# State-space work in short steps between projection blocks, half the output map on GpSimd, and low-part DMAs queued with the low phase

## The chip, the cores and the metric

The kernel runs on one core of one Trainium2 chip. The metric is the device time of one execution in microseconds (us). A core has five engines that each work through a queue of their own in order: TensorE (PE in the profile, its weight loads PEld), VectorE (DVE), ScalarE (ACT), GpSimd (POOL) and SyncE (SP), which here only issues DMAs. An instruction that waits holds up everything behind it on its engine.

## The reference, cut to what matters

One batch of 512 time steps by 1024 channels goes through two layers. Each layer is `x + rms_norm(mixer(rms_norm(x)))`. The change lies in the first layer, whose mixer is:

```python
p = u @ ev_w_in                       # 1024 -> 5120
a_in, a_z, b_val, b_gate, b_z = split(p)          # 1024 columns each
ya = s5_layer(a_in, ...)              # 64 groups of 16 channels, 64 complex states each
ya = gelu(ya); ya = ya * sigmoid(ya @ s5_w_glu + s5_b_glu); ya = ya * silu(a_z)
yb = conformer_conv(b_val, b_gate, ...)           # val*sigmoid(gate), causal conv of 31 taps,
yb = yb * silu(b_z)                               # LayerNorm, swish, pointwise 1024 x 1024
y = concatenate([ya, yb]) @ ev_w_out
```

The state-space part is, per group, `s_t = Lbar * s_(t-1) + Bbar u_t`, `y_t = Re(C s_t) + D u_t`. The second layer is a chunked gated linear attention, which the change leaves alone. Everything is float32.

## The kernel before

**Blocks.** A projection block makes 128 output channels for all 512 steps: 24 matmuls of 128x512 (`mm_st`). Float32 accuracy comes from splitting weights and activations into a high and a low part. A block has a high phase (`wh` times high and low activation, 16 matmuls, L186 and L187) and then a low phase (`wl` times the high activation, 8 matmuls, L189). The first layer's input map has 40 such blocks: 8 for the state-space input (called a here), 8 values (v), 8 gates (g), and 8 each of the two branch gates (zb, za).

**Weights.** For each block SP loads the raw weight (`wraw`, L118, three buffers). ACT writes its negative into `wl` (L130, three buffers), a DMA issued by POOL adds `wraw` to the rounded high part that is still to be taken off (L131, an accumulating DMA, called the low-part DMA here), and ACT makes `wh` (L143, two buffers). ACT also empties the blocks' PSUM banks (three) and issues nothing; a block can start when its `wh` is there and its low phase when the low-part DMA has landed.

**State-space chunks.** The 64 groups go in 8 chunks of 8. `s5_prep(c)` makes a chunk's matrices: the input map `bmt` and `bm` (three two-input operations by `outer`, L528, L530, L532, for each of two halves, on DVE for chunks 0 and 1 and on POOL for the others; then transposes, L544), the response `kt` (L551, L554, L555, L557), the output map `cme` (`outer` again, on DVE, both halves), and for each second chunk the phases (`phases`, six operations on POOL, L507 to L509). It loads `cb` (L519), and ACT makes `csp` and `ci` of it (L522, L523; one `ci` buffer). `s5_in(c)` loads the chunk's input `u` and runs the scan on DVE (L588 to L615), `s5_out(c)` multiplies out `ya` (L628 to L643). The parameters behind all chunks (`s5_params`, powers in `pr`, `prb`, `wb`) are worked out at the start, the last of them on POOL (L398 to L401).

**Order.** A scheduler lays out every engine's queue from priorities and from times that it simulates; `feed()` raises a priority, `background()` lowers it (for the convolution, 31 operations of DVE per chunk, L655 and L656). The program's order sets the rest: 8 a blocks, then `s5_prep` of chunks 0 and 1 and `s5_in(0)`, and then eight rounds. Round c runs `s5_in(c+1)`, `s5_prep(c+2)` and `s5_out(c)` in turn and then four blocks: v, g, zb, za of channel block c. After the rounds come the half-GLU map, the convolution's LayerNorm (it ends in `xbh`), the pointwise map and the output map, and the second layer.

Of the kernel before, what the change touches and what calls it, by code (L numbers as in the profile page):

```python
# [51 lines left out]
def trunk(ctx: ExitStack, tc: tile.TileContext, A: dict, out: bass.AP, dbg: dict | None = None):  # L52
# [58 lines left out]
    wst = {"next_raw": 0, "next_split": 0, "raw": {}, "hl": {}, "low": {}}  # L111
# [10 lines left out]
    def w_low(i, dst=None):  # L122


        while wst["next_raw"] <= i:
            w_raw()
        l = wpool.tile([P, 1024], F32R, tag="wl", bufs=3, name=f"wl{i}") if dst is None else dst
        raw = wst["raw"][i]
        with feed():
            SC.activation(l, raw, AF.Copy, scale=-1.0)  # L130
            G.dma_start(l.bitcast(F32), raw, accum_op=ALU.add)  # L131
        wst["low"][i] = l

    def w_split(dst=None):
        i = wst["next_split"]
        while wst["next_raw"] <= i:
            w_raw()
        if i in dma_low and i not in wst["low"]:
            w_low(i, dst and dst[1])
        raw = wst["raw"].pop(i)  # L140
        h = wpool.tile([P, 1024], F32R, tag="wh", bufs=2, name=f"wh{i}") if dst is None else dst[0]
        with feed():
            SC.copy(h, raw)  # L143
# [23 lines left out]
    def w_get():  # L167
        i = wcur[0]
# [12 lines left out]
    def mm_st(acc, w, xh, xl):  # L181
        wh, wl = w
        whv = wh.rearrange("p (k c) -> p k c", c=P)
        wlv = wl.rearrange("p (k c) -> p k c", c=P)
        for k in range(KT):
            PE.matmul(acc, whv[:, k, :], xh[:, k, :], start=(k == 0), stop=False)  # L186
            PE.matmul(acc, whv[:, k, :], xl[:, k, :], start=False, stop=False)  # L187
        for k in range(KT):
            PE.matmul(acc, wlv[:, k, :], xh[:, k, :], start=False, stop=(k == KT - 1))  # L189
# [96 lines left out]
    SY.dma_start(par, A["s5p"])  # L286
# [205 lines left out]
    def phases(c):  # L492

        sh = [P, GC, 8, 8]
        ws = slice(c // 2 * GC, c // 2 * GC + GC)
# [8 lines left out]
        for o, (a, b, op) in enumerate(((0, 1, ALU.subtract), (1, 0, ALU.add))):
            r_ = h5.tile(sh, F32, tag=f"ph{o}", bufs=1, name=f"ph{o}_{c}")
            wt = h5.tile(sh, F32, tag="wt", bufs=1, name=f"wt{o}_{c}")
            G.tensor_tensor(out=r_, in0=w1(0), in1=w0(a), op=ALU.mult)  # L507
            G.tensor_tensor(out=wt, in0=w1(1), in1=w0(b), op=ALU.mult)
            G.tensor_tensor(out=r_, in0=r_, in1=wt, op=op)  # L509
            out_.append(r_.rearrange("p g a b -> p (g a b)"))  # L510
        pair[c // 2] = out_

    def s5_prep(c):
# [3 lines left out]
        gs = slice(g0_, g0_ + GC)  # L517
        cb = h5.tile([P, 4, GC, GP], F32, tag="cb", bufs=2, name=f"cb{c}")
        SY.dma_start(cb, A["s5cb"][c])  # L519
# [3 lines left out]
        SC.mul(ci_, cb[:, 1], -1.0)  # L523
# [10 lines left out]
        bm = q5.tile([P, GC, P], F32, tag="bm", bufs=2, name=f"bm{c}")  # L534
        cme = q5.tile([P, GC, TB, GP], F32, tag="cme", bufs=3, name=f"cme{c}")
        kt = q5.tile([P, GC, GP], F32, tag="kt", bufs=2, name=f"kt{c}")
        for h in range(2):
            hs = slice(h * 4, h * 4 + 4)
            bmt = q5.tile([P, 4, GP, TB], F32, tag="bmt", bufs=2, name=f"bmt{c}")
            pt1 = h5.tile([P, 4, GP, TB], F32, tag="wt", bufs=1, name=f"pt1_{c}")  # L540
            outer(pe_, bmt, pt1, h, prb, cb[:, 2, hs], cb[:, 3, hs], 2)
            tp = ps("aux")
            for j in range(4):
                PE.transpose(tp[:, j * P:(j + 1) * P], bmt[:, j].rearrange("p q s -> p (q s)"), ident)  # L544
            with feed():
                SC.copy(bm[:, hs, :], tp.rearrange("p (g n) -> p g n", n=P))
            yield

            kp = ps("aux")
            for j in range(4):  # L550
                PE.matmul(kp[32 * j:32 * j + 32, 0:P], cr_[:, h * 4 + j, :], bmt[:, j].rearrange("p q s -> p (q s)"), start=True, stop=True)  # L551
            ks = q5.tile([P, P], F32, tag="ks", bufs=2, name=f"ks{c}")
            with feed():
                SC.copy(ks, kp[:, 0:P])  # L554
            PE.transpose(kp[:, P:2 * P], ks, ident)  # L555
            with feed():
                V.tensor_tensor(out=kt[:, hs, :], in0=kp[:, P:2 * P].rearrange("p (g q) -> p g q", q=32)[:, :, 0:GP],  # L557
                                in1=dg[:, g0_ + h * 4:g0_ + h * 4 + 4, :], op=ALU.add)
# [7 lines left out]

        if c % 2 == 0:
            phases(c)
        half = slice(c % 2 * NS, c % 2 * NS + NS)
        ct_, st_ = (h5.tile([P, S], F32, tag=n, bufs=2, name=f"{n}{c}") for n in ("ct", "st"))  # L570
        for dst, src in zip((ct_, st_), pair[c // 2]):
            for r_ in range(2):
                SY.dma_start(dst[r_ * NS:r_ * NS + NS], src[half])
        prep[c] = (bm, cme, tm, ct_, st_)
# [84 lines left out]
    for c in range(KT):  # L659
# [3 lines left out]
        with feed():  # L663
            ai = tmp((P, TB, NB))
            SC.copy(ai, acc.rearrange("p (b s) -> p s b", s=TB))
            SY.dma_start(u_d[c], ai)

    def value_gate(c):
        w = w_get()
        av = ps()  # L670
        mm_st(av, w, uh, ul)
        w = w_get()
        ag = ps()
        mm_st(ag, w, uh, ul)
        h = hpool.tile([P, 30 + S], F32, tag="h", name=f"h{c}")
        G.memset(h[:, 0:30], 0.0)
        with feed():
            sg = tmp()
            SC.activation(sg, ag, AF.Sigmoid)  # L679
            V.tensor_mul(h[:, 30:30 + S], av, sg)  # L680
        htile[c] = h
        with background():
            conv(c)
# [3 lines left out]
    def gate_z(dst):  # L687
        w = w_get()
        acc = ps()
        mm_st(acc, w, uh, ul)  # L690
        with feed():
            sg = tmp()
            SC.activation(sg, acc, AF.Silu)
            SY.dma_start(dst, sg)

    def run(g, n=1):
        for _ in range(n):
            next(g)

    for c in range(2):  # L700
        run(s5_prep(c), 5)
    run(s5_in(0), 2)
    for c in range(KT):
        nx = s5_in(c + 1) if c + 1 < KT else iter([None] * 2)
        pre = s5_prep(c + 2) if c + 2 < KT else iter([None] * 5)
        cur = s5_out(c)
        run(nx)
        run(pre, 2)
        run(nx)
        run(cur)  # L710
        run(pre, 2)
        run(cur)
        run(pre)
        value_gate(c)
        gate_z(zb_d[c])
        gate_z(za_d[c])
# [500 lines left out]
```

## Time and profile before

| | us |
|---|---|
| median of 3 executions | 945.14 (944.32 to 946.32) |
| the profiled execution, its own time | 946.38 |
| span of its profile | 944.7 |
| PE busy | 897.7 (95%) |
| DVE busy | 641.9 (68%) |
| ACT busy | 485.1 (51%) |
| POOL busy | 245.4 (26%) |

A row of the timeline is the start, the duration, the engine, the line, and the tiles, with the idle time of the engine just before and what ended it in brackets. A row of a table by windows is the stretch of time, its length, the busy time of the engines named, the TensorE clock granted (1.00 is full speed), the mean share of the 16 DMA engines, and the bytes they moved. A row of a table of waits names who waited for what: the total, how often, and the longest. Stages of PE's work, by its own rows: the first 8 blocks run from 17 to 64.24 us, the blocks and chunks of the rounds from there to 320.10, the half-GLU map and the beginning of the output map up to 413.00, then the pointwise map, the rest of the output map, and the second layer.

### The profile page before, as it was taken

The page shows a single profiled execution, that of the slowest core. Times are in us where ns is not written, and L with a number is a line of the kernel's source. Part 1 is how long each engine was busy: PE and PEld are TensorE (multiplying, and loading weights), DVE is VectorE, ACT ScalarE, POOL GpSimd, SP SyncE. Part 2 cuts the span into 40 slices and gives each one's busy share as a digit, 9 for nine tenths or more (in the row PEclk, how much of TensorE's full clock was granted, in tenths as well). Part 3 has the DMA queues.
Part 4 walks back from the last instruction along what each step waited for, and adds up shares of the span by engine and source line. Part 5 has one row for each costly group of instructions (what it writes and reads, how often), then busy time and mean ns, then how long its engine had stood idle before and what let it go on. Part 6 is the DMA issues. An engine that isn't in the chain of part 4 may idle for free. (4 is left out here: it accounts for less than half of the span.)

```text
span 944.7 us, 12134 instructions
## 1 busy us (share of the span) xinstructions
PE 897.7 (95%) x4396; PEld 718.9 (76%) x4396; DVE 641.9 (68%) x1206; ACT 485.1 (51%) x693; POOL 245.4 (26%) x258
## 2 busy tenths in 40 slices
PE   5995998999999999999999979999999999999996
PEld 4873776777778877778887758888888888888875
DVE  7953999999989989832579477584483232744546
ACT  6542786786678855564444566343543242523430
POOL 2693657463123422011054002000200020000222
PEclk8998999999999999999999979999999999999998
DMA  9877987787988885288463112212212223324412
GB/s 278 228 198 194 229 199 184 178 205 204 215 220 228 210 231 179 92 224 201 153 215 124 45 63 93 84 37 82 90 67 90 73 83 135 134 89 164 193 45 89
DMA packets 54955, 142.74 MB, mean 151 GB/s; under 512 B 14256, under 2 KB 15792, under 8 KB 54896
## 3 DMA queue, kind: packets, MB, share of 16 engines
q1 hardware_dynamic: 46832, 112.62, 35.9%
q0 software_dynamic: 8064, 29.36, 17.3%
q8 instruction: 34, 0.56, 0.2%
q14 instruction: 25, 0.20, 0.1%
HBM read 95.18 MB, written 13.22 MB: 115 GB/s over the span
## 5 line engine op out<-in xcount | busy, mean ns | idle before, releaser
L143 ACT CAST wh<-wraw 128x1024 fp32r<-128x1024 f32 x126 | 132.1, 1048 | 161.4 <-PE ps_mm L801 92.5
L149 DVE TENSOR_TENSOR wl<-wraw,wh 128x1024 fp32r<-128x1024 f32 x70 | 87.0, 1243 | 115.2 <-ACT wh L143 114.8
L655 DVE SCALAR_TENSOR_TENSOR ps_cv<-h,cw,ps_cv 128x512 f32<-128x512 f32 x232 | 161.7, 745 | 2.7 <-ACT ps_cv L652 1.8
L186 PE MATMUL ps_mm<-u0h,wh 128*128 128x512 f32 x320 | 129.9, 407 | 1.0 <-ACT tmp L679 0.7
L187 PE MATMUL ps_mm<-u0l,wh 128*128 128x512 f32 x320 | 129.4, 405 | 0.0
L800 PE MATMUL ps_mm<-wh,u1h 128*128 128x512 f32 x240 | 96.2, 402 | 3.5 <-ACT wh L143 3.4
L801 PE MATMUL ps_mm<-wh,u1l 128*128 128x512 f32 x240 | 96.3, 401 | 0.8 <-DVE u1l L194 0.8
L131 POOL DMA_DIRECT2D wl<-wraw x56 | 48.9, 884 | 182.4 <-ACT wl L130 178.2
L802 PE MATMUL ps_mm<-wl,u1h 128*128 128x512 f32 x240 | 91.6, 401 | 1.6 <-DVE wl L149 1.6
L189 PE MATMUL ps_mm<-u0h,wl 128*128 128x512 f32 x320 | 82.5, 395 | 1.1 <-DMA wl<-wraw 1.1
L186 PEld LDWEIGHTS ps_mm<-u0h,wh 128*128 128x128 f32 x320 | 61.8, 193 | 16.4 <-issue 1.6
L130 ACT ACTIVATE wl<-wraw 128x1024 fp32r<-128x1024 f32 x56 | 59.2, 1057 | 25.8 <-DMA wraw<-in_w_in_dram 14.0
L187 PEld LDWEIGHTS ps_mm<-u0l,wh 128*128 128x128 f32 x320 | 61.7, 193 | 13.9 <-issue 1.1
L189 PEld LDWEIGHTS ps_mm<-u0h,wl 128*128 128x128 f32 x320 | 59.4, 188 | 14.9 <-DMA wl<-wraw 1.5
L800 PEld LDWEIGHTS ps_mm<-wh,u1h 128*128 128x128 f32 x240 | 45.9, 191 | 14.9 <-ACT wh L143 3.8
L971 POOL TENSOR_TENSOR rg<-rg,ng 128x512 f32<-128x512 f32 x16 | 24.2, 1544 | 124.6 <-ACT rg L970 124.6
L802 PEld LDWEIGHTS ps_mm<-wl,u1h 128*128 128x128 f32 x240 | 45.6, 191 | 13.1 <-DVE wl L149 2.3
L801 PEld LDWEIGHTS ps_mm<-wh,u1l 128*128 128x128 f32 x240 | 45.9, 191 | 11.7 <-DVE u1l L194 1.2
L186 PE MATMUL ps_mm<-u1h,wh 128*128 128x512 f32 x128 | 50.7, 396 | 0.0
L187 PE MATMUL ps_mm<-u1l,wh 128*128 128x512 f32 x128 | 50.5, 394 | 0.0
L1062 POOL TENSOR_TENSOR kr<-kr,fac 128x384 f32<-128x384 f32 x8 | 6.7, 837 | 124.2 <-DVE rr L205 65.1
L800 PE MATMUL ps_mm<-wh,oth 128*128 128x512 f32 x96 | 37.8, 396 | 0.5 <-ACT wh L143 0.5
(341 smaller groups left out, 1993.6 us busy)
## 6 DMA issues: line engine op xcount, KB each, us to landing
wl<-wraw POOLq DMA_DIRECT2D x56, 512.0 KB, 6.1
wraw<-in_w_in_dram SPq DMA_DIRECT2D x40, 512.0 KB, 5.2
wraw<-in_w_out_dram SPq DMA_DIRECT2D x32, 512.0 KB, 3.3
wraw<-in_w_vr_dram SPq DMA_DIRECT2D x32, 512.0 KB, 3.2
wraw<-in_w_qk_dram SPq DMA_DIRECT2D x16, 512.0 KB, 3.3
tm<-kt_d SPq DMA_DIRECT2D x8, 512.0 KB, 6.3
wraw<-in_w_glu_dram SPq DMA_DIRECT2D x8, 512.0 KB, 5.8
wraw<-in_w_pw_dram SPq DMA_DIRECT2D x8, 512.0 KB, 5.1
```

The costliest lines, as they stand in the source:

```text
L130: SC.activation(l, raw, AF.Copy, scale=-1.0)
L131: G.dma_start(l.bitcast(F32), raw, accum_op=ALU.add)
L143: SC.copy(h, raw)
L149: V.tensor_tensor(out=l, in0=raw, in1=h.bitcast(F32), op=ALU.subtract)
L186: PE.matmul(acc, whv[:, k, :], xh[:, k, :], start=(k == 0), stop=False)
L187: PE.matmul(acc, whv[:, k, :], xl[:, k, :], start=False, stop=False)
L189: PE.matmul(acc, wlv[:, k, :], xh[:, k, :], start=False, stop=(k == KT - 1))
L655: V.scalar_tensor_tensor(out=acc, in0=h[:, k:k + S], scalar=cw[:, c, k:k + 1], in1=acc, op0=ALU.mult, op1=ALU.add)
L800: PE.matmul(accs[tt], xh[:, kt, ts_], whj, start=(first and j == 0), stop=False)
L801: PE.matmul(accs[tt], xl[:, kt, ts_], whj, start=False, stop=False)
L802: PE.matmul(accs[tt], xh[:, kt, ts_], wlj, start=False, stop=(last and j == 1))
L971: G.tensor_tensor(out=r_, in0=r_, in1=ng, op=ALU.mult)
```

## The change

1. The blocks' order. It was a0 to a7 and then v, g, zb, za per round. It is now a0, a1, v0, g0, a2 to a7, zb0, za0, and then v, g, zb, za for the channel blocks 1 to 7.
2. `s5_prep` is cut into six steps (first input map; its transposes and the `ci` and `csp` of ACT; the response, second input map, first output map; turned response, second transposes, phases; second response, second output map, loading the phases; second turned response and `tm`), and `s5_in` gets a step of its own for its load. After six blocks these steps run one block apart; then come rounds with 2, 2, 2, 3, 3, 4, 4, 4 blocks.
3. The second half of the output map is made by GpSimd for chunks 2 to 7 (three operations a chunk).
4. The low-part DMA is ordered behind the last matmul of a block's high phase. The dependency is one of order for the scheduler; it adds no semaphore.
5. Cosine and sine of the phases share a tile, so two DMAs of 64x1024 load them for a chunk where four of 64x512 did.
6. The state-space parameters are loaded between the second and the third tile of x, not behind the vectors.
7. `ci` has two buffers, the response and the turned response a PSUM bank each.

```diff
+    order0 = [("a", 0), ("a", 1), ("v", 0), ("g", 0)] + [("a", j) for j in range(2, 8)] + [("zb", 0), ("za", 0)]
+    for j in range(1, 8):
+        order0 += [("v", j), ("g", j), ("zb", j), ("za", j)]
...
         with feed():
-            SC.activation(l, raw, AF.Copy, scale=-1.0)
-            G.dma_start(l.bitcast(F32), raw, accum_op=ALU.add)
+            SC.activation(l, wst["raw"][i], AF.Copy, scale=-1.0)
         wst["low"][i] = l
+        wst["add"].append((i, l, wst["raw"][i]))
+
+    def w_add(after=None):
+
+        for i, l, raw in wst["add"]:
+            with feed():
+                d = G.dma_start(l.bitcast(F32), raw, accum_op=ALU.add)
+            if after is not None:
+                tc.add_manual_dep(d.ins, after.ins.name, mybir.DependencyInfo(mybir.DependencyClass.NoSync, mybir.DependencyReason.DATA), reason="w_add")
+        wst["add"] = []
...
-            PE.matmul(acc, whv[:, k, :], xl[:, k, :], start=False, stop=False)
+            last = PE.matmul(acc, whv[:, k, :], xl[:, k, :], start=False, stop=False)
+        w_add(last)
...
         SY.dma_start(x_t[tt], A["x"][tt * P:(tt + 1) * P, :])
+        if tt == 1:
+            SY.dma_start(par, A["s5p"])
...
-        ci_ = h5.tile([P, GC, GP], F32, tag="ci", bufs=1, name=f"ci{c}")
...
+        def output_map(h):
+            eng = G if h and c >= DVE_PREP else V
+            pt2 = h5.tile([P, 4, TB, GP], F32, tag="wt", bufs=1, name=f"pt2_{c}") if eng is G else q5.tile([P, 4, TB, GP], F32, tag="pt", bufs=1, name=f"pt2_{c}")
+            outer(eng, cme[:, hs[h]], pt2, h, pr, cr_[:, hs[h], 0:GP], ci_[:, hs[h]], 3)
+
+        input_map(0)
+        yield
...
+        ci_ = h5.tile([P, GC, GP], F32, tag="ci", bufs=2, name=f"ci{c}")
+        turn(0)
+        SC.activation(cr_[:, :, 0:GP], cb[:, 0], AF.Copy, scale=sgn)
+        SC.mul(ci_, cb[:, 1], -1.0)
+        yield
...
+        ks = response(0)
+        input_map(1)
+        output_map(0)
+        yield
+        turn_response(0, ks)
+        turn(1)
+        if c % 2 == 0:
+            phases(c)
+        yield
+        ks = response(1)
+        output_map(1)
...
+    blocks(6)
+    run(P_[0])
+    blocks()
+    run(P_[0])
+    blocks()
+    run(P_[0])
+    blocks()
+    run(P_[0], P_[1], I_[0])
+    blocks()
+    run(P_[0], P_[1])
+    blocks()
+    run(P_[0], I_[0], P_[1])
+    blocks()
+    run(I_[0], P_[1])
+    blocks(2)
+    run(P_[1], P_[2], I_[1])
+    blocks(2)
     for c in range(KT):
...
+        n = (2, 2, 2, 3, 3, 4, 4, 4)[c]
+        run(O_[c], nx, p1, p2)
+        blocks(n - n // 2 - n // 3)
+        run(nx, p2, O_[c])
+        blocks(n // 3)
+        run(p2)
+        blocks(n // 2)
+        run(p2, p3)
+        if c + 2 < KT:
+            run(I_[c + 2])
```

Three places show what this does to the queues. The first is POOL's queue at the start, where the low-part DMAs (wl3 belongs to the fourth block) stand among the parameter work (`ya`, `s5ph` and `wb` are its tiles). Before:

```order
L131 DMA wl2_478<-wraw2_469 128x1024
L131 DMA wl3_513<-wraw3_476 128x1024
L398 TENSOR_TENSOR ya_87<-s5ph1_350 128x64
L399 TENSOR_TENSOR ya_87<-s5ph1_350 128x64
L131 DMA wl4_548<-wraw4_511 128x1024
L400 TENSOR_TENSOR s5ph2_351<-ya_87 128x32
L401 TENSOR_TENSOR s5ph2_351<-ya_87 128x32
```

Of the change, from eight operations further on in the same parameter work:

```order
L410 TENSOR_TENSOR ya_87<-s5ph4_352 128x64
L411 TENSOR_TENSOR ya_87<-s5ph4_352 128x64
L412 TENSOR_TENSOR wb_96<-ya_87 128x32
L136 DMA wl3_529<-wraw3_492 128x1024
L413 TENSOR_TENSOR wb_96<-ya_87 128x32
L410 TENSOR_TENSOR ya_87<-wb_96 128x64
L411 TENSOR_TENSOR ya_87<-wb_96 128x64
L136 DMA wl4_564<-wraw4_527 128x1024
L412 TENSOR_TENSOR wb_96<-ya_87 128x32
```

The DMA of wl3 was ahead of the parameter work and stands 11 operations into it. The same holds a block later for wl5 (before behind the second L398 and L399 on `wb`, now ten operations later) and for wl6 and wl7.

The second place is POOL's queue in the middle of the rounds, where it makes phases (`ph`, `wt`) and the input maps (`bmt3`). Before:

```order
L509 TENSOR_TENSOR ph0_2_1065<-ph0_2_1065,wt0_2_1066 128x512
L508 TENSOR_TENSOR wt1_2_1071<-wb_96 128x512
L131 DMA wl13_1221<-wraw13_1184 128x1024
L509 TENSOR_TENSOR ph1_2_1070<-ph1_2_1070,wt1_2_1071 128x512
L530 TENSOR_TENSOR pt1_3_1274<-prb_95,cb3_1265 128x512
L131 DMA wl14_1384<-wraw14_1219 128x1024
L528 TENSOR_TENSOR bmt3_1273<-prb_95,cb3_1265 128x512
```

Of the change:

```order
L520 TENSOR_TENSOR ph2_1421<-ph2_1421,wt0_2_1422 128x512
L519 TENSOR_TENSOR wt1_2_1426<-wb_96 128x512
L136 DMA wl17_1254<-wraw17_1217 128x1024
L520 TENSOR_TENSOR ph2_1421<-ph2_1421,wt1_2_1426 128x512
L535 TENSOR_TENSOR pt2_2_1506<-pr_94,ci2_1323 128x512
L537 TENSOR_TENSOR cme2_1384<-cme2_1384,pt2_2_1506 128x512
L535 TENSOR_TENSOR pt1_3_1516<-prb_95,cb3_1513 128x512
L533 TENSOR_TENSOR cme3_1624<-pr_94,csp1_455 128x512
```

The operations on `cme` are the half of the output map that DVE had. They stand between the phases and the input map of the next chunk, and chunk 2 gets there four blocks later than before (wl17 for wl13).

The third place is ACT's queue around the `ci` of chunk 3, which needs the load of `cb3`. Before:

```order
L554 COPY ks0_818<-ps_aux_813 128x128
L522 ACTIVATE csp0_454<-cb2_956,sgn_74 128x8x16
L546 COPY bm1_850<-ps_aux_858 128x512
L130 ACTIVATE wl11_1117<-wraw11_1083 128x1024
L523 ACTIVATE ci3_1267<-cb3_1265 128x128
L143 CAST wh11_1182<-wraw11_1083 128x1024
L554 COPY ks1_869<-ps_aux_864 128x128
```

Of the change:

```order
L128 ACTIVATE wl12_961<-wraw12_900 128x1024
L562 COPY ks0_938<-ps_aux_933 128x128
L583 ACTIVATE csp0_454<-cb2_1206,sgn_74 128x8x16
L553 COPY bm1_947<-ps_aux_949 128x512
L584 ACTIVATE ci3_1560<-cb3_1513 128x128
L152 CAST wh12_1027<-wraw12_900 128x1024
L723 ACT_TABLE_LOAD
L723 ACTIVATE tmp_989<-ps_mm_963 128x512
```

Both queues have `ci3` directly ahead of a weight's high part, wh11 before and wh12 in the change (blocks are counted from 0). The response copy `ks1` stood right behind them; in the change it comes after another emptied block.

More of the change, by code (lines that the diff above doesn't have):

```diff
@@ L110, in trunk @@
                     wlist.append(A["w_out1"][n, (h - 2) * 4 + j])
-    wst = {"next_raw": 0, "next_split": 0, "raw": {}, "hl": {}, "low": {}}
+    wst = {"next_raw": 0, "next_split": 0, "raw": {}, "hl": {}, "low": {}, "add": []}
     def w_raw():
@@ L139, in w_split @@
             w_low(i, dst and dst[1])
+        if any(a[0] == i for a in wst["add"]):
+            w_add()
         raw = wst["raw"].pop(i)
@@ L167, in w_get @@
     def w_get():
+        w_add()
         i = wcur[0]
@@ L532, in outer, with input_map, turn, response @@
             eng.tensor_tensor(out=o, in0=o, in1=pt, op=ALU.add)
[L534 to L538, printed above, removed]
+        hs = [slice(0, 4), slice(4, 8)]
+        bmts = []
+        def input_map(h):
             bmt = q5.tile([P, 4, GP, TB], F32, tag="bmt", bufs=2, name=f"bmt{c}")
             pt1 = h5.tile([P, 4, GP, TB], F32, tag="wt", bufs=1, name=f"pt1_{c}")
-            outer(pe_, bmt, pt1, h, prb, cb[:, 2, hs], cb[:, 3, hs], 2)
+            outer(pe_, bmt, pt1, h, prb, cb[:, 2, hs[h]], cb[:, 3, hs[h]], 2)
+            bmts.append(bmt)
+        def turn(h):
             tp = ps("aux")
             for j in range(4):
-                PE.transpose(tp[:, j * P:(j + 1) * P], bmt[:, j].rearrange("p q s -> p (q s)"), ident)
+                PE.transpose(tp[:, j * P:(j + 1) * P], bmts[h][:, j].rearrange("p q s -> p (q s)"), ident)
             with feed():
-                SC.copy(bm[:, hs, :], tp.rearrange("p (g n) -> p g n", n=P))
-            yield
+                SC.copy(bm[:, hs[h], :], tp.rearrange("p (g n) -> p g n", n=P))
+        def response(h):
             kp = ps("aux")
             for j in range(4):
-                PE.matmul(kp[32 * j:32 * j + 32, 0:P], cr_[:, h * 4 + j, :], bmt[:, j].rearrange("p q s -> p (q s)"), start=True, stop=True)
+                PE.matmul(kp[32 * j:32 * j + 32, 0:P], cr_[:, h * 4 + j, :], bmts[h][:, j].rearrange("p q s -> p (q s)"), start=True, stop=True)
             ks = q5.tile([P, P], F32, tag="ks", bufs=2, name=f"ks{c}")
@@ L565, in s5_prep @@
         SY.dma_start(tm, bass.AP(tensor=kd.tensor, offset=kd.offset, ap=[[(2 * TB - 1) * P, GP], [P, TB], [1, TB * P]]))
[L567 to L574, printed above, removed]
+        tms[c] = tm
         yield
+    tms = {}
     state = {}
@@ L615, in s5_in @@
         V.tensor_tensor(out=sv[:, :, 1:NB], in0=zv[:, :, 0:NB - 1], in1=zsv[:, :, 0:NB - 1], op=ALU.subtract)
-        state[c] = (u, sv, tm, cme)
+        state[c] = (u, sv, cme)
         yield
     def s5_out(c):
-        u, sv, tm, cme = state.pop(c)
+        (u, sv, cme), tm = state.pop(c), tms.pop(c)
         yp_ = ps("aux")
@@ L656, in conv, with block @@
         V.scalar_tensor_tensor(out=h[:, 30:30 + S], in0=h[:, 30:30 + S], scalar=cw[:, c, 30:31], in1=acc, op0=ALU.mult, op1=ALU.add)
-    for c in range(KT):
+    half_glu = {}
+    def block(n, c):
         w = w_get()
@@ L662, in trunk @@
         mm_st(acc, w, uh, ul)
[L663 to L683, printed above, removed]
@@ L685, in trunk @@
-    za_d, zb_d = ([dram.tile([P, S], F32, name=f"z{n}_d{c}") for c in range(KT)] for n in "ab")
[L687 to L696, printed above, removed]
-        for _ in range(n):
[L698 to L702, printed above, removed]
-    for c in range(KT):
[L704 to L716, printed above, removed]
+        if n == "a":
+            with feed():
+                ai = tmp((P, TB, NB))
+                SC.copy(ai, acc.rearrange("p (b s) -> p s b", s=TB))
+                SY.dma_start(u_d[c], ai)
+        elif n == "v":
+            half_glu[c] = acc
+        elif n == "g":
+            h = hpool.tile([P, 30 + S], F32, tag="h", name=f"h{c}")
+            G.memset(h[:, 0:30], 0.0)
+            with feed():
+                sg = tmp()
+                SC.activation(sg, acc, AF.Sigmoid)
+                V.tensor_mul(h[:, 30:30 + S], half_glu.pop(c), sg)
+            htile[c] = h
+            with background():
+                conv(c)
+        else:
+            with feed():
+                sg = tmp()
+                SC.activation(sg, acc, AF.Silu)
+                SY.dma_start((za_d if n == "za" else zb_d)[c], sg)
@@ new lines, in trunk, with blocks, run @@
+    za_d, zb_d = ([dram.tile([P, S], F32, name=f"z{n}_d{c}") for c in range(KT)] for n in "ab")
+    todo = iter(order0)
+    def blocks(n=1):
+        for _ in range(n):
+            b = next(todo, None)
+            if b:
+                block(*b)
+    def run(*gs):
+        for g in gs:
+            next(g, None)
+    P_ = [s5_prep(c) for c in range(KT)]
+    I_ = [s5_in(c) for c in range(KT)]
+    O_ = [s5_out(c) for c in range(KT)]
+    none = iter(())
+    blocks(6)
+    run(P_[0])
+    blocks()
```

53 lines of the change are left out of this document (28 added, 25 removed).

## The prediction

> **What bounds the kernel now.** I begin with the page's busy line and then look at PE by stages, because its share is highest.
>
> ```profile
> PE 897.7 (95%) x4396; PEld 718.9 (76%) x4396; DVE 641.9 (68%) x1206; ACT 485.1 (51%) x693; POOL 245.4 (26%) x258
> ```
> The windows of PE, cut at the end of the eighth block, the start of the half-GLU map and the start of the pointwise map, where the change ends (columns: stretch, length, PE busy, clock, DMA share, GB/s):
> ```profile
> 17.00:64.24 47.24, 46.15 (x193) 0.96 0.84 213
> 64.24:320.10 255.86, 237.84 (x1458) 0.97 0.82 204
> 320.10:413.00 92.90, 91.93 (x389) 1.00 0.64 178
> ```
> The first layer's rounds are the one stage that the change reorders where PE is idle for long: 255.86 − 237.84 = 18.0 us, and the clock is below full. PE's waits in that stage:
> ```profile
> PE ps_aux L555 <- ACT ks L554: 10.4, 1, 10.4
> PE ps_aux L551 <- DVE kt L557: 4.2, 3, 1.8
> PE ps_aux L588 <- DMA u<-u_d: 1.7, 1, 1.7
> PE ps_aux L544 <- ACT ya L643: 0.9, 1, 0.9
> PE ps_mm L186 <- ACT tmp L679: 0.7, 1, 0.7
> ```
> They sum to 17.9 us. One wait makes up most of it. ACT's, PE's and SP's timelines show how it comes about:
> ```profile
> 91.28 0.31 ACT L523 ACTIVATE ci<-cb 128x128 f32<-128x128 f32 x1 [8.99 <-DMA cb<-in_s5cb_dram]
> ```
> ```profile
> 92.74 0.48 PE L555 MATMUL ps_aux<-ident,ks 128*128 128x128 f32 x1 [10.38 <-ACT ks L554]
> ```
> ```profile
> 85.81 0.58 SPq L519 DMA_DIRECT2D cb<-in_s5cb_dram  x1
> ```
> The load of `cb` was issued at 85.81 and ACT's `ci` waited for it until 91.28; `ks`, which PE needed, was queued behind. It is an in-order jam, not a shortage of ACT. The clock pays again behind it. Two windows of PE (columns as above):
> ```profile
> 93.00:96.00 3.00, 3.00 (x10) 0.50 0.78 262
> 180.00:185.00 5.00, 4.66 (x20) 0.66 1.02 218
> ```
> Half speed for about 3.4 us (92.7 to 96.1; and 0.66 over five microseconds is 5 × 0.34 / 0.5 = 3.4 us of half speed) loses 1.7 us each time, 3.4 us in all.
>
> **The floor of the stage.** Undisturbed, a block takes 5.49 us, read from the starts of low phases one block apart:
> ```profile
> 50.05 1.99 PE L189 MATMUL ps_mm<-u0h,wl 128*128 128x512 f32 x8
> ...
> 55.55 1.99 PE L189 MATMUL ps_mm<-u0h,wl 128*128 128x512 f32 x8
> ...
> 62.30 2.10 PE L189 MATMUL ps_mm<-u0h,wl 128*128 128x512 f32 x8 [1.09 <-DMA wl<-wraw]
> ```
> 32 blocks from the ninth on take 175.7 us. 255.86 − 175.7 − 17.9 − 3.4 = 58.9 us is left for the state-space matmuls, 7.4 us a chunk. The change keeps these matmuls, so 175.7 + 58.9 = 234.6 us is what the stage needs if nothing waits. **Gain term: −21.3 us** (255.86 to 234.6). In the new order `ks1` is no longer behind `ci3`, `ci` has two buffers, and `u` is loaded a step ahead. wh12 is behind `ci3` instead, with about 4 us to spare by the same load time.
>
> **The cost at the start.** POOL's timeline of before:
> ```profile
> 38.75 0.89 POOL L131 DMA_DIRECT2D wl<-wraw  x1
> ...
> 48.19 0.88 POOL L131 DMA_DIRECT2D wl<-wraw  x1
> ...
> 56.93 0.88 POOL L131 DMA_DIRECT2D wl<-wraw  x1
> ...
> 64.19 0.85 POOL L131 DMA_DIRECT2D wl<-wraw  x1
> ...
> 67.59 1.29 POOL L509 TENSOR_TENSOR ph<-ph,wt 128x512 f32<-128x512 f32 x1
> ```
> and from the row of the `wl` tiles in the first 110 us:
> ```profile
> DMA to landing us min/median/max: 4.7/5.3/8.6
> ```
> The DMAs at 38.75, 48.19, 56.93 and 64.19 are those of blocks 5 to 8 (counted from 0). Block 7's landed too late: 56.93 + 5.3 = 62.2, the start of its low phase at 62.30. In the change each stands about one place further back in the same parameter work: block 5's just ahead of where block 6's was, block 6's where block 7's was, block 7's where block 8's was, block 8's behind the operation at 67.59. From those times I take off 1.0 to 1.6 us, because the operations of the DMAs that no longer stand ahead (0.6 us from one start to the next) and some fills fall away. This gives issues of 46.6 (block 5), 55.9 (6), 63.2 (7) and 67.2 (8). Landed 5.3 us later, block 6's is there at 61.2, where the low phase wants it at 55.5 + 1.0 (matmuls start 1 us later, below): a stall of 4.7 us. Block 7's is there at 68.5 and wanted 5.49 us after 61.2, at 66.7: 1.8 us. Block 7 then ends at 68.5 + 1.9 = 70.4 and not at 64.24. **Start term: +6.1 us**, with 0 as one end (a place in the order is no time) and, with the longest landing of 8.6, 9.4 as the other. Block 8's lands at 72.5, before its low phase at 74.1.
>
> The earlier load of the parameters puts 25 small operations of DVE ahead of the last scaling of x, for which PE's transposes wait; 6 stood there before.
> ```profile
> 22.33 0.41 DVE L324 TENSOR_SCALAR s5t<-s5t 128x64 f32<-128x64 f32 x3
> ```
> 19 more at 0.41 / 3 = 0.14 us are 2.6 us, some of it in DVE's own waiting for x. I take 1.0 us (0 to 2.6), already within the 6.1.
>
> **DVE in the rounds.** The next question is whether DVE lets PE have 234.6 us. Two windows, all engines (PE, PEld, DVE, ACT, POOL):
> ```profile
> 97.00:165.00 68.00, 62.83 (x431) 48.41 (x428) 66.70 (x89) 48.89 (x72) 44.00 (x36) 1.00 0.82 200
> 165.00:320.10 155.10, 152.62 (x902) 120.28 (x901) 150.24 (x224) 116.47 (x152) 55.63 (x50) 0.99 0.83 205
> ```
> DVE is busy for 217 of 223 us, and that was hidden because most of it is convolution that can wait until the half-GLU stage. The rows of DVE's pace:
> ```profile
> 299.55 9.30 DVE L655 SCALAR_TENSOR_TENSOR ps_cv<-h,cw,ps_cv 128x512 f32<-128x512 f32 x14
> 308.77 0.68 DVE L194 TENSOR_TENSOR yal<-ya,yah 128x512 fp32r<-128x512 f32 x1
> 309.37 0.74 DVE L655 SCALAR_TENSOR_TENSOR ps_cv<-h,cw,ps_cv 128x512 f32<-128x512 f32 x1
> ...
> L608 DVE TENSOR_TENSOR_SCAN zb<-rv,za x7: 1206/1212/2092, 109.0 to 254.3; 128x512 f32<-128x512 f32 x7
> ...
> L528 DVE TENSOR_TENSOR cme<-pr,csp 128x512 f32<-128x512 f32 x10 | 9.2, 955 | 0.0
> ```
> A convolution operation takes 9.22 / 14 = 0.66 us, a two-input one 0.60 to 0.62, a scan 1.2, and beside POOL's work a two-input operation takes 0.96. Between the first operation of chunk 1's scan and that of chunk 7's, six rounds, the new order has 116 convolution operations, 51 two-input ones, 6 scans and 11 small `kt`: 76.6 + 31.6 + 7.2 + 1.4 = 116.8 us, and with nine operations a round lengthened by 0.3 us, 133 us. PE has 16 blocks and six chunks there: 87.8 + 44.4 = 132.2 us. So DVE has no room left in the rounds, and where the scan's result is wanted within a block PE will wait a little. **Waits term: +4 us**, from 0 (as long as DVE overlaps well) to 12 (two microseconds a round, the longest `kt` wait being 1.8).
>
> **The output map on GpSimd.** The 18 operations (three for each of chunks 2 to 7) leave DVE at 0.61 to 0.96 us each, 11 to 17 us, which the counts above already leave out. POOL's groups between 97 and 265 us:
> ```profile
> L528 POOL TENSOR_TENSOR bmt<-prb,cb 128x512 f32<-128x512 f32 x11 | 15.7, 1429 | 10.2 <-PE ps_aux L551 10.2
> L530 POOL TENSOR_TENSOR pt<-prb,cb 128x512 f32<-128x512 f32 x10 | 13.0, 1304 | 0.8
> L509 POOL TENSOR_TENSOR ph<-ph,wt 128x512 f32<-128x512 f32 x6 | 9.3, 1550 | 0.2
> ```
> and over the whole run
> ```profile
> L528 POOL TENSOR_TENSOR bmt<-prb,cb x12: 1059/1366/2112, 84.2 to 224.1; 128x512 f32<-128x512 f32 x12
> ```
> They cost POOL about 1.4 us each. If DVE's two-input operations are shut out for that time, DVE gets back 18 × 1.4 = 25 us of waiting for some 16 us of work, 9 us more than nothing. [...] The trace agrees in part: 955 ns beside POOL's work against 0.60 alone, which is far from a whole POOL operation each time.
>
> POOL's own load: nine operations a chunk and three of phases on the mean, 12 × 1.4 = 16.8 us, with 3 DMAs × 0.6 18.6 us, against PE's 22 us a round. It fits.
>
> **Behind the stage.** DVE's last convolution and the LayerNorm behind it:
> ```profile
> 361.14 0.74 DVE L656 SCALAR_TENSOR_TENSOR h<-h,cw,ps_cv 128x512 f32<-128x512 f32 x1
> ...
> 408.27 0.60 ACT L193 CAST xbh<-ln 128x512 fp32r<-128x512 f32 x1
> ...
> 413.00 0.47 PE L186 MATMUL ps_mm<-xbh,wh 128*128 128x512 f32 x1 [0.88 <-ACT wh L143]
> ```
> `xbh` is ready 4.1 us before PE needs it. An earlier end of the rounds would make it late, but the convolution begins earlier too: channel block 0 is the third and fourth block now and falls into DVE's long idle times,
> ```profile
> 68.92 0.69 DVE L530 TENSOR_TENSOR pt<-prb,cb 128x512 f32<-128x512 f32 x1 [10.17 <-POOL ph L509]
> ...
> 91.62 0.69 DVE L530 TENSOR_TENSOR pt<-pr,ci 128x512 f32<-128x512 f32 x1 [14.03 <-ACT ci L523]
> ```
> 24 us, as much as the 31 operations of a channel block (20.5 us). I count nothing behind the stage. Without that cover an end 11.2 us earlier would leave `xbh` 11.2 − 4.1 = 7.1 us late. The second layer has the same instructions. The merged phase loads and the PSUM banks cost nothing on a path: they end long before the scan that uses them.
>
> **Sum.** Stage end 320.10 + 6.1 − 21.3 = 304.9, with the waits 308.9. The span becomes 944.7 − 11.2 = 933.5. The profiled execution lies 946.38 − 944.7 = 1.7 above its span, so 935.2, and it was 1.24 above the median of 945.14: against the median **934.0 us**, 1.2% faster. A measurement of this kernel can tell about 0.2% from no change, which is 943.25 to 947.0.
>
> **The rivals.**
> - *Forecast, 0.52:* 934, between 929 and 940.
> - *Everything fits, 0.12:* no stall at the start beyond before's and no waits of DVE, 934.0 − 6.1 − 4 = 924. For it: list order isn't time. Against it: block 7's low part already came late.
> - *The shut-out of DVE, 0.10:* the 9 us above lie on a DVE without room, 943. Against it: 955 ns.
> - *The jam moves, 0.11:* the change takes the wait away in one place and gets it back behind another load in ACT's or SP's queue, such as `ci3` ahead of wh12: 10.4 + 1.7 us more than forecast, 946. For it: `cb` still waits behind a raw weight in SP's queue. The change then does not do what it says.
> - *GpSimd becomes the bound, 0.15, slower:* at 2.11 us, the longest in the row above, 12 operations and the DMAs take 27.1 us a round, and PE's 22.0 are no longer the limit: 6 × 5.1 = 31 us on 304.9, stage end 336, time 961. It decides from (22 − 1.8) / 12 = 1.7 us for a mean operation, and operations come near it if DVE's own lengthen them; the means of before are 1.3 to 1.55.
>
> [...] After a wait as long as block 6's (4.7 us) the clock can fall, as it did after 10.38 us; a half-speed stretch of 3.4 us costs 1.7 us, which block 7's own wait of 1.8 us would hide. [...]
>
> **How the numbers follow.** Likeliest 934.0. Faster holds the first three cases, 0.74; same is the moved jam, 0.11; slower GpSimd, 0.15. The range leaves out the slower case and the very end of the good one: 924 to 946.
>
> **What would show it.** The start: block 7 ends near 70 with waits for `wl<-wraw` of some 6 us. The gain: no wait above 3 us between there and the half-GLU map, which begins near 309. The waits: `kt`, `sv` and `gs` releases of PE summing to about 4 us. DVE: two-input operations no longer than 0.96 on the mean. POOL: operations of the rounds at 1.3 to 1.55 and no PE wait ending on `bmt` or `cme` of POOL. If POOL's means pass 1.7, or a wait of 10 us stands in the rounds again, the prediction is wrong.

## The result, and the profile after

The change made the kernel slower: 953.72 us (median of 4 executions, 950.88 to 953.94) against 945.43 us before, a ratio of 1.0078 with a 95% interval of 1.0057 to 1.0099. The forecast was 934.0 us with a range of 924 to 946. The profiled execution took 953.63 us, with a span of 951.9 us, 7.2 us more than the span of before. One execution of all those below, of e_early, took 4992.51 us; the ratios leave it out.

The windows of PE after the change, cut at the same events as before (end of the eighth block, start of the half-GLU map, start of the pointwise map, end); columns are stretch, length, PE busy, clock, DMA share, GB/s:

```profile
19.10:68.60 49.50, 47.30 (x199) 1.00 0.74 186
68.60:324.10 255.50, 236.14 (x1453) 0.97 0.83 206
324.10:418.96 94.86, 91.94 (x390) 1.00 0.64 177
418.96:951.90 532.94, 515.27 (x2328) 0.98 0.34 110
```

The eighth block ends at 68.60 and not at 64.24: 4.4 us later. The rounds take 255.50 us where they took 255.86: 0.4 us less. The stage of the half-GLU map takes 94.86 for 92.90, 2.0 us more, and the rest of the span 532.94 for 944.70 − 413.00 = 531.70, 1.2 us more. 4.4 − 0.4 + 2.0 + 1.2 = 7.2. The rounds, where 17.3 us net were to be won, gave nothing.

PE's waits in the rounds after the change:

```profile
PE ps_aux L633 <- ACT gs L629: 7.4, 1, 7.4
PE ps_mm L200 <- DMA wl<-wraw: 3.2, 2, 1.6
PE ps_aux L666 <- DVE sv L653: 2.2, 2, 1.2
PE ps_aux L666 <- DVE ps_cv L693: 2.1, 1, 2.1
PE ps_aux L551 <- POOL bmt L537: 1.4, 1, 1.4
PE ps_aux L626 <- DVE kt L569: 1.4, 1, 1.4
PE ps_mm L196 <- ACT tmp L715: 0.8, 1, 0.8
```

With two smaller ones (0.6 and 0.2) they sum to 19.3 us. The single wait of 10.4 us became one of 7.4 us, and the small ones grew from 7.5 us to 11.9. The timelines of SP, ACT and PE show that the long one is the old jam again, with the same load in front of the same operation:

```profile
93.58 1.33 SPq L528 DMA_DIRECT2D cb<-in_s5cb_dram  x1
```
```profile
100.94 0.31 ACT L584 ACTIVATE ci<-cb 128x128 f32<-128x128 f32 x1 [12.32 <-DMA cb<-in_s5cb_dram]
...
104.94 0.58 ACT L629 COPY gs<-ps_aux 128x512 f32<-128x512 f32 x1
```
```profile
105.57 1.11 PE L633 MATMUL ps_aux<-ident,gs 128*128 128x128 f32 x4 [7.41 <-ACT gs L629]
```

The load of `cb` for chunk 3 is issued at 93.58, where it was issued at 85.81 before. ACT stands at `ci` for 12.32 us until 100.94, and then works off four operations before it reaches `gs`, which PE needs. PE then runs at half speed for some 3.5 us, as the first of these windows shows, which loses another 1.7 us:

```profile
105.50:109.00 3.50, 3.43 (x13) 0.50 0.84 157
```
```profile
242.00:247.00 5.00, 4.49 (x15) 0.66 1.02 232
252.00:257.00 5.00, 5.00 (x51) 0.66 0.78 152
```

The other two windows stand over 130 us behind the jam. Each holds 5 × 0.34 / 0.5 = 3.4 us of half speed, the one behind the wait of 1.4 us for `bmt` and the other behind that of 2.1 us for `ps_cv`. So the rounds lost three times 1.7 us, 5.1 us, to the clock, where the kernel before lost 3.4.

### The profile page after: what moved, and what is told of

The parts are those of the page before. It is cut to its first block, busy times and chain, and to the rows that moved or that the text cites. A ratio compares the mean times of both kernels' runs of the same rounds, so it can differ in the third digit from the quotient of the medians.

```text
span 951.9 us, 12093 instructions
## 1 busy us (share of the span) xinstructions
PE 898.5 (94%) x4396; PEld 721.1 (76%) x4396; DVE 637.5 (67%) x1188; ACT 487.1 (51%) x694; POOL 263.8 (28%) x276
## 4 chain that ended last, share of the span: by engine, by line
PE 62%; DVE 19%; DMA 7%; ACT 5%; issue 3%; POOL 3%; SPq 1%; DVEq 0%; POOLq 0%; ACTq 0%
PE ps_mm L863 9%; PE ps_mm L862 9%; PE ps_mm L861 9%; DVE ps_cv L693 9%; PE ps_mm L196 8%; PE ps_mm L197 8%; PE ps_mm L200 7%; PE ps_aux L1139 2%; DMA wl<-wraw 2%; DMA cb<-in_s5cb_dram 1%; DMA cs<-ph 1%; DMA wraw<-in_w_out_dram 1%; PE ps_mm L955 1%; PE ps_mm L956 1%; PE ps_mm L959 1%
## 5 line engine op out<-in xcount | busy, mean ns | idle before, releaser
L693 DVE SCALAR_TENSOR_TENSOR ps_cv<-h,cw,ps_cv 128x512 f32<-128x512 f32 x232 | 168.8, 750 | 5.0 <-ACT ps_cv L690 1.9
```

The lines of the kernel that those rows point to most:

```text
L693: V.scalar_tensor_tensor(out=acc, in0=h[:, k:k + S], scalar=cw[:, c, k:k + 1], in1=acc, op0=ALU.mult, op1=ALU.add)
```

## The experiments

All ratios are to the kernel before, which ran on the same chip beside each batch (medians 946.73, 946.10 and 945.51 us). Differences are given in us at 946 us.

### Four edits one at a time: which part costs, and what feeds the jam

**x_hold** keeps the phases of chunk 2 from standing ahead of low-part DMAs on POOL. In the changed kernel POOL waits there for the loads out of the phases' one buffer, and two low-part DMAs stand behind:

```profile
82.15 2.10 POOL L518 TENSOR_TENSOR ph<-wb 128x512 f32<-128x512 f32 x2 [13.80 <-DMA cs<-ph]
84.20 1.79 POOL L136 DMA_DIRECT2D wl<-wraw  x2
```

```diff
-    def phases(c):
+    def phases(c, after=None):
...
-            G.tensor_tensor(out=cs[:, o], in0=w1(0), in1=w0(a), op=ALU.mult)
+            first = G.tensor_tensor(out=cs[:, o], in0=w1(0), in1=w0(a), op=ALU.mult)
+            if after is not None:
+                tc.add_manual_dep(first.ins, after.ins.name, mybir.DependencyInfo(mybir.DependencyClass.NoSync, mybir.DependencyReason.DATA), reason="ph_hold")
...
-            phases(c)
+            phases(c, t1 if c >= 2 else None)
```

Here `t1` is the last of the chunk's second transposes.

> The change with one more order: the first phase operations of chunk 2 (and 4, 6) on GpSimd stand behind chunk 2's own transposes, so behind the low-part DMAs wl10 to wl19 instead of ahead of wl10. Theory Q (a chain through the queues): in the changed kernel POOL's first phase operation of chunk 2 waits 13.8 us for the four loads of the phases, the DMAs of wl10 and wl11 stand behind it, the raw weights on SP wait for those, the load of cb3 is behind the raw weights, and ACT's ci3 waits 12.3 us for it and holds gs, for which PE waits 7.4 us. Then here wl10 is issued about 13 us earlier (near 71 and not 84.2), ci3 waits under 4 us, PE's wait for gs is gone with its half clock: 943 to 945 us. Theory L (the new place of the low-part DMAs itself is the cost, ci3 would wait anyway): ci3 still waits over 8 us, the time stays within 2 us of 953.7.

Measured: ratio 1.0098 (1.0059 to 1.0136), no gain, as theory L had it. The first link of theory Q did as it should, the last did not. The timelines of POOL, ACT and PE:

```profile
72.18 0.85 POOL L136 DMA_DIRECT2D wl<-wraw  x1 [4.11 <-ACT ks L565]
87.29 0.85 POOL L136 DMA_DIRECT2D wl<-wraw  x1 [14.26 <-PE ps_mm L197]
```
```profile
85.93 1.06 ACT L128 ACTIVATE wl<-wraw 128x1024 fp32r<-128x1024 f32 x1 [8.92 <-DMA wraw<-in_w_in_dram]
...
99.60 0.31 ACT L587 ACTIVATE ci<-cb 128x128 f32<-128x128 f32 x1 [8.82 <-DMA cb<-in_s5cb_dram]
```
```profile
104.22 1.11 PE L636 MATMUL ps_aux<-ident,gs 128*128 128x128 f32 x4 [6.75 <-ACT gs L632]
```

The low-part DMA behind the phases goes out at 72.18 and not at 84.20, but `ci` still gets its load only at 99.60, and PE waits 6.75 us. The next low part had to wait for a raw weight on ACT until 85.93. So theory Q fell: POOL's wait of 13.8 us is not what makes the load of `cb` late.

**e_early** undoes the fourth part.

```diff
         wst["add"].append((i, l, wst["raw"][i]))
+        w_add()
```

> The change with its fourth part undone: the low-part DMA is queued right behind ACT's operation again. Theory L: the four waits of PE for wl (7.4 us in all) fall under 2 us and the jam at ci3 goes with them: 944 to 947 us. Theory Q: only the direct waits of blocks 7 and of the half-GLU map go (2.2 and 2.0 us), ci3 still waits over 8 us and PE for gs over 4 us: 948 to 951 us.

Measured: ratio 1.0046 (1.0023 to 1.0069), 3.0 us less than the change by the ratios, whose intervals overlap. PE's waits in its first 425 us:

```profile
PE ps_aux L634 <- ACT gs L630: 7.7, 1, 7.7
PE ps_mm L201 <- DMA wl<-wraw: 6.7, 5, 2.4
```

The jam is there in full (7.7 us), so theory L fell as a cause of it. (This profile is of the fastest of the run's executions, 947.02 us.) The waits for the low parts are 6.7 us where they were 7.4, so they hardly hang on where the DMA is queued either.

**e_dvemap** undoes the third part (`eng = V` for both halves of the output map).

> The change with its third part undone: both halves of the output map on DVE again. Theory C (DVE and GpSimd get in each other's way): PE's waits for DVE and POOL between 165 and 324 us (7.6 us in the changed kernel) fall under 3 us: about 948 us. Theories Q and L: the 18 operations are back on a DVE without room, waits there do not fall, 954 us or up to 8 us more; the jam at ci3 is as before.

Measured: ratio 1.0078 (1.0049 to 1.0108), the same as the change. PE's waits in its first 425 us:

```profile
PE ps_aux L633 <- ACT gs L629: 7.4, 1, 7.4
PE ps_aux L666 <- DVE ps_cv L693: 4.7, 1, 4.7
...
PE ps_aux L666 <- DVE sv L653: 3.1, 1, 3.1
```

In the stretch that the expectation names, 165 to 324 us, the waits for DVE and POOL did fall, from 7.6 to 3.1 us, nearly as theory C has it. But the wait for `ps_cv` stands just ahead of that stretch, at 155 us, and with it PE waits 7.8 us for DVE; the time is not the 948 us of theory C. So theory C fell by its time and not by its sign.

**e_par** undoes the sixth part.

```diff
-        if tt == 1:
-            SY.dma_start(par, A["s5p"])
     SY.dma_start(vec, A["vec"])
     w_raw()
+    SY.dma_start(par, A["s5p"])
```

> The change with its sixth part undone: the state-space parameters are loaded behind the vectors again. All theories: the first block's matmuls start near 17.0 us and not 19.1, 2.1 us less: 951.6 us if the start is on the path; if block 7's low part sets the pace there (parameter work on POOL, now later), block 7 still ends near 68.5 and the time stays 953.7.

Measured: ratio 1.0040 (1.0013 to 1.0068), 3.6 us less than the change by the ratios. Its profiled execution started the first block at 17.78 us; the jam was there with `ci` waiting 8.8 us. The intervals of e_par and of the change overlap.

### Taking the jam out

**f_cb** gives the half of `cb` that ACT reads a tile of its own, with three buffers, loaded one chunk ahead. Nothing else of the program changes.

```diff
-        cb = h5.tile([P, 4, GC, GP], F32, tag="cb", bufs=2, name=f"cb{c}")
-        SY.dma_start(cb, A["s5cb"][c])
+        for c_ in ([0, 1] if c == 0 else [c + 1]):
+            if c_ < KT:
+                ca_[c_] = h5.tile([P, 2, GC, GP], F32, tag="ca", bufs=3, name=f"ca{c_}")
+                SY.dma_start(ca_[c_], A["s5cb"][c_][:, 0:2])
+        cb = h5.tile([P, 2, GC, GP], F32, tag="cb", bufs=2, name=f"cb{c}")
+        SY.dma_start(cb, A["s5cb"][c][:, 2:4])
...
-        SC.activation(cr_[:, :, 0:GP], cb[:, 0], AF.Copy, scale=sgn)
-        SC.mul(ci_, cb[:, 1], -1.0)
+        SC.activation(cr_[:, :, 0:GP], ca_[c][:, 0], AF.Copy, scale=sgn)
+        SC.mul(ci_, ca_[c][:, 1], -1.0)
```

> The change, but what ACT needs of cb (its first half, for csp and ci) is a tile of its own with three buffers, loaded one chunk ahead, so that ca3 is issued on SP ahead of the raw weight of block 7 and not behind that of block 14. Theory J (the jam at ci3 is what ate the gain): ACT does not wait for ci3, PE's wait for gs (7.4 us) and the half-clock stretch behind it (1.7 us) are gone: 943 to 946 us. Theory D (the DMA engines are full there, and cb3 is one late load among several): PE waits instead for the weights of blocks 11 to 13 (wh, wl), which x_hold showed landing at 86 us: at most 3 us are won, 951 to 953 us.

Measured: 942.89 us, ratio 0.9963 (0.9939 to 0.9987). That is 1.15% or 10.9 us below the change by the ratios. SP issues chunk 3's half at 40.72, ACT copies `gs` at 94.57, ten microseconds earlier than in the changed kernel, and no wait for it is left among PE's waits in the rounds:

```profile
40.72 0.89 SPq L532 DMA_DIRECT2D ca<-in_s5cb_dram  x1
```
```profile
94.57 0.57 ACT L635 COPY gs<-ps_aux 128x512 f32<-128x512 f32 x1
```
```profile
PE ps_aux L672 <- DVE sv L659: 4.5, 3, 2.2
PE ps_mm L200 <- DMA wl<-wraw: 4.3, 3, 2.1
PE ps_aux L672 <- DMA tm<-kt_d: 3.5, 1, 3.5
PE ps_aux L557 <- DVE za L648: 1.7, 1, 1.7
PE ps_aux L632 <- DVE kt L575: 1.4, 1, 1.4
```

Theory J holds and theory D fell. POOL still waited 13.25 us for the phases' loads in this run, which says once more that that wait alone costs nothing. The other half of `cb` still left SP only at 93.35 us, so the edit did not make SP's line faster; it took out of it what ACT needs. But 15.4 us of small waits between 60 and 320 us are still there (2.1 of them are block 7's low part).

**f_bcb** makes the same single edit in the kernel before.

> The kernel before with the same single edit (first half of cb in three buffers, a chunk ahead). Theory J: the wait of 10.4 us and 1.7 us of half clock go, 12 us faster than before, ratio 0.987. Theory D: the weights of blocks 11 and 12 are late in its place, at most 4 us faster, ratio 0.996 or more.

Measured: 938.73 us, ratio 0.9913 (0.9893 to 0.9933): 8.2 us won where the wait and its clock were 12.1. The long wait is gone, and some smaller ones are larger than they were (`kt` by 2.3 us, `u` by 0.6 and `ya` by 0.7):

```profile
PE ps_aux L557 <- DVE kt L563: 4.2, 4, 1.7
PE ps_aux L550 <- DVE kt L563: 2.3, 1, 2.3
PE ps_aux L594 <- DMA u<-u_d: 2.3, 1, 2.3
PE ps_aux L550 <- ACT ya L649: 1.6, 1, 1.6
```

**f_cbep** is f_cb with the fourth and sixth part undone.

> The change with the edit of f_cb and with its fourth and sixth part undone (low-part DMAs right behind ACT's operation, parameters loaded behind the vectors). Theory J: 938 to 941 us, faster than before. Theory D: 946 to 948 us.

Measured: 938.73 us, ratio 0.9904 (0.9882 to 0.9926). It beats both kernels, as f_bcb does, and cannot be told from f_bcb.

**e_earlypar** undoes the fourth and sixth part and leaves the jam in.

> The change with its fourth and its sixth part undone, the jam left in. If the two parts cost what their single undoing showed (3 and 3.5 us) and add up: ratio to before 1.000 to 1.002, PE's waits for wl under 3 us in all. If both pay for the same late low part of block 7: ratio 1.004, as each alone.

Measured: ratio 1.0025 (1.0002 to 1.0048), between the two expectations and not apart from either; `gs` waited 6.5 us, and PE's waits for wl came to 3.8 us.

### The parts again, without the jam

**g_cbp** is f_cb with the sixth part undone.

> f_cb with the sixth part undone (parameters loaded behind the vectors). If the earlier parameters cost the start itself: first block's matmuls near 17.6 us and not 19.8, the 2.2 us kept to the end, ratio to before 0.994 (f_cb had 0.9963). If block 7's late low part takes them back: 0.996.

Measured: ratio 0.9936 (0.9910 to 0.9961), 2.6 us less than f_cb by the ratios. PE's first block of the change, of f_cb and of g_cbp:

```profile
19.12 0.80 PE L196 MATMUL ps_mm<-u0h,wh 128*128 128x512 f32 x1 [0.61 <-DVE u0l L317]
```
```profile
19.79 0.50 PE L196 MATMUL ps_mm<-u0h,wh 128*128 128x512 f32 x1 [1.14 <-DVE u0l L317]
```
```profile
17.10 0.50 PE L196 MATMUL ps_mm<-u0h,wh 128*128 128x512 f32 x1 [0.35 <-DVE u0l L316]
```

The start moves by 2 to 2.7 us, and the ratios agree with it being kept to the end, though the intervals of g_cbp and f_cb overlap.

**g_cbe** is f_cb with the fourth part undone.

> f_cb with the fourth part undone (low-part DMAs right behind ACT's operation). f_cb and f_cbep differ by 0.6%, 2.2 us of which the sixth part would be; the rest, 3.4 us, falls to the fourth if the two add up: ratio 0.9925, PE's waits for wl under 4 us (f_cb has 6.2). If the place of the DMA is of no account once ci3 does not jam: 0.996.

Measured: ratio 0.9963 (0.9940 to 0.9986), the same as f_cb. PE's waits for wl stayed at 6.3 us in its first 425 us (6.2 in f_cb), not under 4. Without the jam the new place of the low-part DMA costs nothing that can be measured.

**g_cbepd** is f_cbep with the third part undone too.

> f_cbep with the third part undone too (the whole output map on DVE). If the move to GpSimd relieves DVE: the 18 operations are back, 12 us on a DVE that is busy all the time, PE waits for DVE 2 to 6 us longer, ratio 0.993 to 0.997 (f_cbep 0.9904). If GpSimd's work takes as much from DVE as it relieves: within 0.002 of f_cbep.

Measured: ratio 0.9916 (0.9896 to 0.9937), within 0.0012 of f_cbep. The half output map on GpSimd relieves nothing that the time shows. DVE's operations on the map with half of it (f_cbep) and with all of it (g_cbepd), in groups between 100 and 290 us:

```profile
L543 DVE TENSOR_TENSOR cme<-cme,pt 128x512 f32<-128x512 f32 x5 | 7.2, 1448 | 0.0
L541 DVE TENSOR_TENSOR pt<-pr,ci 128x512 f32<-128x512 f32 x4 | 7.1, 1786 | 0.0
L539 DVE TENSOR_TENSOR cme<-pr,csp 128x512 f32<-128x512 f32 x5 | 6.2, 1247 | 0.7 <-POOL ph L520 0.7
```
```profile
L539 DVE TENSOR_TENSOR cme<-pr,csp 128x512 f32<-128x512 f32 x10 | 11.4, 1182 | 0.0
L543 DVE TENSOR_TENSOR cme<-cme,pt 128x512 f32<-128x512 f32 x10 | 9.3, 931 | 0.0
L541 DVE TENSOR_TENSOR pt<-pr,ci 128x512 f32<-128x512 f32 x9 | 9.0, 1004 | 0.0
```

14 operations took 20.5 us (1.46 each) with GpSimd's share beside them, 29 took 29.7 us (1.02 each) without. So 15 operations fewer saved 9.2 us of the 15.4 that they cost at 1.02. In the same views three two-input groups of the scan, of 8 operations each (L649, L650, L655), took 23.8 us with GpSimd's share and 17.9 without. In this pair DVE pays back most of what it hands over, on the operations that it keeps.

**g_bcbg** is f_bcb with the third part alone.

> f_bcb (the kernel before without the jam) with the third part alone: second half of the output map of chunks 2 to 7 on GpSimd. If it relieves DVE: PE's waits for kt (6.5 us in f_bcb) fall by half, ratio 0.988 (f_bcb 0.9913). If GpSimd and DVE hold each other up, or POOL's in-order queue delays bmt and the low-part DMAs: 0.991 to 0.995.

Measured: ratio 1.0031 (1.0012 to 1.0051), worse than either expectation. The profiled execution was 12.6 us longer than that of f_bcb, but part of it was lost before any moved operation had run (the first is at 81.53 us): block 7 waited for its low part, on an unchanged queue,

```profile
66.36 3.54 PE L189 MATMUL ps_mm<-u0h,wl 128*128 128x512 f32 x8 [4.02 <-DMA wl<-wraw]
```

where f_bcb waited 0.93 us. Another 2.97 us are a low part in the half-GLU stage. Half speed made up a good part of the rest: g_bcbg's profile has four such stretches, near 20, 66, 124 and 188 us, where f_bcb's has a granted clock of 1.00 in every window from 60 to 325 us (on the mean of the whole executions 0.985 against 0.990). In those near 66 and 124 us the eight low-phase matmuls of a block took 3.54 and 3.58 us, against 1.99 undisturbed, 1.6 us more each; by that I estimate the loss of the four together at about 6 us. How much of the 11 us belongs to the third part, and why the early part of it comes, is left open.

## Why the prediction was wrong, point by point

**The gain term (−21.3 us) failed, and with it the forecast.** Its floor was not the trouble: the profile after shows 19.3 us of waits and 5.1 us of half clock in 255.50 us, which leaves 231.1 us of work where the forecast had 234.6, and part of that difference is PE work that now runs ahead of the eighth block's end (47.30 us busy there for 46.15). What failed is the sentence that the jam would be gone, because "wh12 is behind `ci3` instead, with about 4 us to spare by the same load time". The load time was not the same: `cb` was issued 7.8 us later and landed 7.3 us after its issue, 9.7 us later on ACT than before. I had looked at what stood behind `ci3` on ACT and left the load's own place on SP, behind raw weights, as it was before. Nor did I follow ACT's queue to the operation that PE came to want first, which was not wh12 but `gs`, four operations further back. By the old load time it would still have done: `gs` was ready 4.6 us after `ci` began, so at 95.9 us with `ci` at 91.28, and PE wanted it at 98.2 (an estimate from the rows above). f_cb shows the price: taking this one load out of SP's line wins 10.9 us and turns the change from slower to faster than before.

**The clock in the gain term.** It counted both half-speed stretches of before, 3.4 us, as gone. The one at 180 us stood behind a wait of only 1.66 us (`kt`, at 180.34), and the forecast left waits of that size in. After the change there were three stretches, two of them behind waits of 1.4 and 2.1 us; other waits of that size have none behind them (1.53 us at 74.42, 1.62 at 88.84 and 2.04 at 346.86 after the change, with a granted clock of 1.00 in the microseconds that follow), so it is not settled what decides. By this the term was 5.1 us too large, the jam's own 1.7 among them.

**The rival of the moved jam** named this very place and was given 0.11 and 946 us. The mechanism was right; it was priced against a kernel that had won everything else. It belonged into the forecast, since its own text says that "`cb` still waits behind a raw weight in SP's queue".

**The start term (+6.1 us)** was roughly right as a sum: 4.4 us measured. Its division was not. The scaling of x, put at 1.0 of 0 to 2.6 us, cost 2.1 in the profile of the change, and the sixth part is where single undoing shows it, with and without the jam (3.6 and 2.6 us by the ratios, whose intervals overlap). Block 6 did not stall; block 7 waited 2.17 us.

**The waits term (+4 us)** was too small. Without `gs` and the low parts, 8.7 us of small waits for DVE, POOL and ACT stood in the rounds; in f_cb, too, waits for `sv`, `za` and `kt` made 7.6 us. The bound of 12 held.

**The low parts in the rounds** (3.2 us) and in the half-GLU stage (2.0 us) had no term. Undoing the fourth part did not remove them.

**The output map on GpSimd** was costed as relief of 11 to 17 us against lengthening. In the new order the runs show no net effect (1.0078 against 1.0078 with the jam, 0.9904 against 0.9916 without). In the old order the part alone came with a loss of 11.2 us (g_bcbg), of which the runs do not show how much is its own. DVE's own operations on the map went to 1.46 us on the mean in f_cbep, above the 0.96 that I had taken; in the changed kernel they took 1.28 us for the sum and 1.19 and 0.73 for the two products. Whether DVE is shut out for whole operations of GpSimd, as the rival of that name supposed, or only slowed, no run shows. GpSimd did not become the bound: its three groups of the output map ran at 1.22 to 1.39 us on the mean, and only 1.4 us of PE's waits ended on `bmt`.

**The finer steps (parts 1, 2 and 5, with 7)** were to win by taking the work behind the jam apart. With the jam taken out of both orders and the third, fourth and sixth part undone, the new order (g_cbepd, 0.9916) and the old one (f_bcb, 0.9913) take the same time. So the new order by itself wins nothing that could be measured. Of all that was tried, the one load won most.

**The sum.** The span after is 951.9 us, 18.4 more than the 933.5 of the forecast. In the rounds, 255.50 us stand against 234.6 + 4 = 238.6, 16.9 more: 7.4 for `gs`, 5.1 of half speed, and other waits of 11.9 where 4 were counted, less the 3.5 us by which the work was shorter. The start cost 1.7 us less than the 6.1 counted, and the stages behind the rounds 3.2 us more, which had no term. (The stretch from the pointwise map to the end lasts 529.4 to 533.1 us in the profiles of all the runs, so its 1.2 us may be chance.) The jam with its own half clock, 9.1 us, is thus half of what was missed. f_cb, without it, takes 942.89 us: that is inside the range, but still 8 to 9 us above the forecast.

By the ratios the jam is worth 10.9 us in the changed kernel and 8.2 in the one before. f_cb and f_bcb, both without it, differ by 0.50%, 4.7 us, of which the sixth part is about 2.6. That the 2.7 us between the two jams and these 4.7 add up to the 7.4 measured follows from the arithmetic and shows nothing. The remaining 2 us are not assigned; they lie within the intervals.

What stays open in part is why the raw weights, and behind them `cb`, leave SP so late between 66 and 94 us. Neither POOL's wait for the phases' loads (x_hold) nor the place of the low-part DMA (e_early) is the reason. SP's own waits between 55 and 100 us, after the change and before it, name what it stood for:

```profile
SPq L117 <- DMA wl<-wraw: 22.7, 5, 8.2
```
```profile
SPq L118 <- DMA wl<-wraw: 17.5, 3, 8.8
```

By these rows the three buffers of the raw weights come free when a low-part DMA that reads them has landed, and after the change those took, between 55 and 105 us,

```profile
DMA to landing us min/median/max: 4.5/7.1/11.9
```

Before, the same row had 4.7, 5.3 and 8.6. So the line is held up by low-part DMAs that land later than they did. Why they land later, and whether more buffers for the raw weights would help, was not tried.

## What to carry to other kernels

Where an in-order engine waits for a load, look at when the load is issued and what stands ahead of it in the queue that issues it; moving the work behind the wait here only chose which consumer was late (PE waited 10.38 us for `ks` before and 7.41 us for `gs` after). A small load that several engines hang on, given its own buffers and issued a chunk ahead, won 10.9 us in the changed kernel and 8.2 in the one before, where the reordering of the whole stage won nothing that could be measured (0.9916 against 0.9913); it is worth trying first. When a rival names a concrete instruction that still stands behind the same queue, its place belongs in the forecast until a row shows the load arriving in time.

## What the runs showed that I had not expected

The four loads of the phases took much longer to land in their new form than the first four of the old one, at the same stage of the program. The rows of `cs` (four DMAs of 64x1024, after) and of `ct` (four of 64x512, before), issue to landing:

```profile
DMA to landing us min/median/max: 6.2/9.4/11.5
```
```profile
DMA to landing us min/median/max: 3.3/3.3/6.2
```

SP spent 6.22 us on the four, where the raw weight's DMA just ahead took it 0.33 us; the eight smaller ones of before had taken it 7.6 us. None of PE's waits in the rounds ended on these loads, in the change or in f_cb. What their time at the head of SP's queue cost the raw weights behind them was not tried. In these rows twice the size went with almost three times the time (9.4 against 3.3 us at the median). The four sine loads of before, a little later, took 5.0 us at the median, so part of it may be the crowd of transfers at that time, which is a guess that no run tested.
